# Copies and accumulating transfers of a weight sum moved from the gate and up stage into the attention, and two direct pieces of the down projection moved among the wide pairs

## The chip, the cores and the metric

One core of a Trainium2 chip runs the kernel. The metric is the device time of one execution in microseconds (us). Engines are named as in the profile: PE is TensorE (matmuls; PEld are its weight loads), DVE is VectorE, ACT is ScalarE, POOL is GpSimd, SP is SyncE, which here only issues DMAs. Each engine runs its instructions in the order in which they stand in the program.

## What is computed

One encoder layer over 272 tokens (256 and 16 meta tokens) with two parallel groups of attention heads, then a gated MLP with a depthwise convolution of width 3. In outline, with what doesn't matter here left out:

```python
hn = rmsnorm(h, mix_norm_g)
proj = hn @ w_in                                 # 2048 columns in
q_a, k_a, v_a, cq, ckv, k_pe = split(proj)
out_a = neighbourhood_attention(q_a, k_a, v_a)   # 8 heads of 128
out_b = mla_attention(cq, ckv, k_pe)             # 8 heads, low rank, rotary key
h = h + concat(rmsnorm(out_a), rmsnorm(out_b)) @ w_out
x = rmsnorm(h, ffn_norm_g)
g, u = x @ w_gate, x @ w_up                      # 2048 x 5632 each
gc = conv_b + sum(conv_w[i] * shifted(g, i) for i in range(3))
h = h + (silu(gc) * u) @ w_down                  # 5632 x 2048
return h[N_META:]
```

## The kernel before

Everything is float32. PE multiplies in a shorter format, so each weight tile `raw` is split into a high part `whi` (ACT, line 249) and a low part `wlo` (DVE, line 253, `raw - whi`), and activations likewise (`hl` for hidden states, `act` for MLP values). A product is then two or three matmuls: `mm3` (lines 712 to 714) takes three, `mm2` (lines 2035 and 2036) two, of which the first is 512 columns wide.

Weights come in **pieces** of 128 x 1024 (512 KB), in one list `pieces` that sets the order for the whole kernel: a load on SP into one of five or six `raw` buffers, a split into one of four `whi` and `wlo` buffers, and the products. A `raw` buffer is free when DVE has written `wlo`, and only then SP can issue the next load. The stages by the span's time: input projections and attention to about 285 us, output projection (`w_out`) to about 375, gate and up to about 945, and the down projection to the end; the profile's marks for them are the tile names `in_w_in`, `in_w_out`, `in_w_gate`, `in_w_up` and `in_w_down`.

Parts of up and down use a scheme with seven products for a 2 x 2 block product instead of eight. It needs sums of quarters of the activation, which are saved to DRAM and loaded again (`s_up`, `s_down`, into `sin`, `sums` or a part of `act`), and sums of quarters of the weights (`weight_sums`). `RowPair` is one pair of 128-row blocks in such a group. There are three kinds: five groups of four column tiles in up (`in_w_up_s`), the `mid` group of down (512 columns, `in_w_down_m`), and the **wide group** (the first 1024 columns of down, `in_w_down_s`), with 22 pairs of four pieces each. The last 512 columns of down are **direct pieces** (`others` in the code, `in_w_down` in the profile): four column tiles of 44 blocks, six pieces each, 24 in all, with `mm2` for the first three tiles and `mm3` for the last.

For the wide group one or two of the weight sums are not made by DVE but in DRAM, ahead of time (`early` tiles, 22 of them, 512 KB and 256 KB in turn). For each, SP issues a **copy** of one or two quarters from the weights in DRAM to the tile (line 776), and when that has landed POOL issues an **adding transfer** (line 781) that accumulates another quarter onto it. Both were issued by one generator, `sums_in_dram`, started in `mlp_buffers` at the beginning of gate and up (line 1888). The wide group's pairs then load the tiles like weights.

What sets the order is a planner, `Flow`: each part of the kernel is a generator that asks for an engine with a cost in ns, the planner keeps a clock for each engine, always serves the request that can start first, and writes the instruction into the program at that moment. A transfer is modelled in `load` as bytes at 350 a ns behind all earlier ones (`dma_free`) and a fixed latency. So the order on each engine is fixed when the program is built, and a constant such as `EARLY_PACE`, the planner's pause between two steps of `sums_in_dram`, moves instructions.

The order of the MLP's pieces is the list `work`. Ahead of the wide group's pairs stand the last mid pieces and the first direct pieces, in the order of the string `TAIL` (m is a mid piece, d a direct one); `BEHIND` direct pieces stand behind the pairs, and the rest is spread among them:

```python
    ahead = others[:AHEAD]
    work += [(left if c == "m" else ahead).pop(0) for c in TAIL]
    n = len(others) - BEHIND
    work += spread(scheme, others[AHEAD:n])
    work += others[n:]
```

`spread` puts the last of the pieces that it spreads behind the last pair's piece. After that pair `scheme_out` combines the seven products on ACT, DVE and POOL and sends the result out, while PE works on the direct pieces behind.

## Time and profile before

| | us |
|---|---|
| median of 3 runs | 1115.56 |
| lowest and highest | 1112.71, 1118.1 |
| the profiled execution | 1116.94 |
| its span on the core | 1114.8 |

The span runs from the first to the last instruction of the program; 2.1 us of the execution lie around it. In rows of the profile, `L253 DVE TENSOR_TENSOR wlo<-raw,whi 128x512` is an instruction of line 253 on DVE that writes `wlo` from `raw` and `whi`; buffer numbers are left out. A row with `PE bank L289 <- DVE wlo L253` says that PE's instruction waited, and what it waited for. SPq and POOLq are the issues of DMAs; a `q` behind a number in the DMA view is a hardware queue (q1 is fed by SP, q0 by POOL). Idle time of an engine matters only where PE in the end waits for it.

### The profile page before, as it was taken

How to read it: one execution, taken by the hardware profiler on the slowest of the kernel's cores; microseconds unless marked ns; L12 is line 12 of the kernel's file. 1: busy time of each engine (PE TensorE's matmuls, PEld its weight loads, DVE VectorE, ACT ScalarE, POOL GpSimd, SP SyncE). 2: the span in 40 equal slices, each digit the busy share in tenths (PEclk: the TensorE clock that was granted, in tenths of full speed). 3: DMA queues.
4: the chain of work that ended last, by engine and by line, in shares of the span. 5: the costliest groups of instructions: out<-in, count | busy, mean ns of one | idle time of the engine just before them, and what ended most of it. 6: DMA issues, size and time to landing. Idle time of an engine off the chain costs nothing.

```text
span 1114.8 us, 22339 instructions
## 1 busy us (share of the span) xinstructions
PE 1102.8 (99%) x8164; PEld 1049.1 (94%) x8164; DVE 1015.9 (91%) x1922; ACT 751.8 (67%) x1514; POOL 142.8 (13%) x217
## 2 busy tenths in 40 slices
PE   9999999999999999999999999999999999999998
PEld 9999999999999999999999999999999999887777
DVE  7979888888878989999999999999999989899997
ACT  8788989898647786556656556666665665676664
POOL 3211222121332300000000000000000000310011
PEclk9999999999999999999999999999999999999999
DMA  9653434444655689778868878889889879698891
GB/s 318 197 174 121 151 123 156 139 155 140 225 185 171 216 308 306 250 244 244 288 196 268 253 239 267 284 253 316 296 295 304 269 271 360 241 316 298 296 315 75
DMA packets 82470, 265.35 MB, mean 238 GB/s; under 512 B 9304, under 2 KB 13016, under 8 KB 82360
## 3 DMA queue, kind: packets, MB, share of 16 engines
q1 hardware_dynamic: 78600, 254.08, 66.9%
q0 software_dynamic: 3472, 9.57, 4.9%
q8 instruction: 64, 1.05, 0.4%
q14 instruction: 46, 0.38, 0.1%
q10 hardware_dynamic: 288, 0.27, 0.1%
HBM read 245.39 MB, written 35.13 MB: 252 GB/s over the span
## 4 chain that ended last, share of the span: by engine, by line
PE 62%; DVE 21%; DMA 7%; ACT 5%; issue 4%; POOL 0%; SPq 0%; DVEq 0%; ACTq 0%; POOLq 0%
PE bank L289 14%; DVE wlo L253 12%; PE bank L714 11%; PE bank L712 11%; PE bank L713 11%; PE bank L2035 8%; PE bank L2036 4%; DMA raw<-in_w_up_s 3%; ACT whi L249 3%; DVE raw L253 2%; PE bank L295 2%; DVE mt L253 2%; DMA halves<-early 1%; DVE halves L253 1%; DVE mt L261 1%
## 5 line engine op out<-in xcount | busy, mean ns | idle before, releaser
L249 ACT ACTIVATE whi<-raw 128x512 fp32r<-128x512 f32 (+2 forms) x512 | 381.5, 766 | 159.9 <-PE bank L713 48.1
L253 DVE TENSOR_TENSOR wlo<-raw,whi 128x512 fp32r<-128x512 f32 (+2 forms) x512 | 443.5, 885 | 33.1 <-ACT whi L249 31.7
L712 PE MATMUL bank<-hl,whi 128*128 128x258 f32 (+1 forms) x1208 | 348.5, 289 | 0.1
L714 PE MATMUL bank<-hl,wlo 128*128 128x258 f32 (+1 forms) x1208 | 345.1, 286 | 1.4 <-DVE wlo L253 1.3
L713 PE MATMUL bank<-hl,whi 128*128 128x258 f32 (+1 forms) x1208 | 344.3, 285 | 0.0
L714 PEld LDWEIGHTS bank<-hl,wlo 128*128 128x128 f32 x1208 | 230.4, 191 | 3.5 <-DVE wlo L253 2.9
L713 PEld LDWEIGHTS bank<-hl,whi 128*128 128x128 f32 x1208 | 230.1, 190 | 0.1
L712 PEld LDWEIGHTS bank<-hl,whi 128*128 128x128 f32 x1208 | 229.2, 190 | 0.8 <-ACT scr L249 0.3
L289 PE MATMUL bank<-whi,act 128*128 128x256 f32 (+1 forms) x600 | 153.2, 306 | 0.6 <-ACT whi L249 0.6
L2035 PE MATMUL bank<-hl,whi 128*128 128x512 f32 x384 | 136.5, 395 | 0.0
L289 PEld LDWEIGHTS bank<-whi,act 128*128 128x128 f32 x600 | 105.1, 189 | 7.0 <-ACT whi L249 0.8
L2036 PE MATMUL bank<-hl,wlo 128*128 128x256 f32 x384 | 107.6, 280 | 0.0
L289 PE MATMUL bank<-wlo,act 128*128 128x256 f32 (+1 forms) x300 | 92.3, 308 | 1.4 <-DVE wlo L253 1.4
L2035 PEld LDWEIGHTS bank<-hl,whi 128*128 128x128 f32 x384 | 72.2, 188 | 14.8
L249 ACT ACTIVATE whi<-halves 128x1024 fp32r<-128x1024 f32 (+1 forms) x68 | 63.7, 948 | 32.3 <-PE bank L289 17.5
L253 DVE TENSOR_TENSOR wlo<-halves,whi 128x1024 fp32r<-128x1024 f32 (+1 forms) x68 | 74.1, 1113 | 4.2 <-ACT whi L249 4.2
L289 PE MATMUL bank<-whi,sin 128*128 128x256 f32 (+1 forms) x264 | 76.6, 333 | 0.0
L2036 PEld LDWEIGHTS bank<-hl,wlo 128*128 128x128 f32 x384 | 72.4, 188 | 0.0
L781 POOL DMA_DIRECT2D early<-in_w_down_s x22 | 18.2, 826 | 374.0 <-DMA early<-in_w_down_s 359.4
L249 ACT ACTIVATE whi<-more_raw 128x1024 fp32r<-128x1024 f32 (+2 forms) x59 | 49.6, 856 | 23.2 <-PE bank L2035 7.5
L289 PEld LDWEIGHTS bank<-wlo,act 128*128 128x128 f32 x300 | 56.7, 189 | 5.3 <-DVE wlo L253 2.2
L253 DVE TENSOR_TENSOR wlo<-more_raw,whi 128x1024 fp32r<-128x1024 f32 (+2 forms) x59 | 57.0, 980 | 2.0 <-ACT whi L249 2.0
(309 smaller groups left out, 2151.2 us busy)
## 6 DMA issues: line engine op xcount, KB each, us to landing
raw<-in_w_gate SPq DMA_DIRECT2D x71, 512.0 KB, 5.6
raw<-in_w_in SPq DMA_DIRECT2D x52, 512.0 KB, 4.0
raw<-in_w_up SPq DMA_DIRECT2D x42, 512.0 KB, 5.0
raw<-in_w_up_s SPq DMA_DIRECT2D x33, 512.0 KB, 6.1
raw<-in_w_out SPq DMA_DIRECT2D x32, 512.0 KB, 3.9
sin<-s_down SPq DMA_DIRECT2D x30, 512.0 KB, 7.1
s_down<-sums SPq DMA_DIRECT2D x22, 512.0 KB, 6.9
raw<-in_w_down_m SPq DMA_DIRECT2D x18, 512.0 KB, 6.2
```

The lines of the kernel that those rows point to most:

```text
L249: nc.scalar.activation(out, in_, f, **kw)
L253: nc.vector.tensor_tensor(out, a, b, op)
L261: nc.vector.scalar_tensor_tensor(out, a, s, b, op0, op1)
L289: nc.tensor.matmul(o, l, r, start=start, stop=stop)
L295: nc.tensor.transpose(o, i, ident[:n, :n])
L712: nc.tensor.matmul(ps, whi, xhi, start=start, stop=False)
L713: nc.tensor.matmul(ps, whi, xlo, start=False, stop=False)
L714: nc.tensor.matmul(ps, wlo, xhi, start=False, stop=stop)
L781: nc.gpsimd.dma_start(t, src, accum_op=ALU.add)
L2035: nc.tensor.matmul(ps, whi, x, start=start, stop=False)
L2036: nc.tensor.matmul(ps[:, :n], wlo, x[:, 0, :], start=False, stop=stop)
```

## The change

`sums_in_dram` is split in two. `copies_in_dram` issues the 22 copies on SP with a pause of 6000 in the planner's clock, from when the 15th piece has landed; `sums_in_dram` issues the 22 adding transfers on POOL with a pause of 9500, from when the 49th has. Both are started by `first_loads`, in the attention, and no longer by `mlp_buffers`. The string `TAIL` loses its last d, so 8 and not 9 direct pieces stand ahead of the wide pairs, and `BEHIND` is 3 and not 4, so 13 and not 11 are spread among the pairs. What is computed stays the same.

```diff
-EARLY_PACE = 15000.0
+EARLY_PACE = 9500.0
+COPY_PACE, COPY_AT, SUMS_AT = 6000.0, 14, 48
 LANDING, SAVING = 2600.0, 2500.0
-BEHIND = 4
-MID_LEAD, TAIL = 4, "mmdmmddddmmdddd"
+BEHIND = 3
+MID_LEAD, TAIL = 4, "mmdmmddddmmddd"
...
+    copied = [Event() for _ in early]
+
+    def copies_in_dram():
+        for (t, src, _, _), ev in zip(early, copied):
+            yield "sp", 600
+            load(t, src, ev, nc.sync)
+            fl.cur.t += COPY_PACE
+
     def sums_in_dram():
-        copied = [Event() for _ in early]
-        for i in range(len(early) + 2):
-            if i < len(early):
-                t, src, _, _ = early[i]
-                yield "sp", 600
-                load(t, src, copied[i], nc.sync)
-            if i >= 2:
-                t, _, src, done = early[i - 2]
-                yield copied[i - 2]
-                yield "pool", 1000
-                nc.gpsimd.dma_start(t, src, accum_op=ALU.add)
-                dma_free[0] = max(dma_free[0], fl.cur.t) + 8 * P * size(t) / 350.0
-                fl.set(done, 8000.0)
+        for (t, _, src, done), ev in zip(early, copied):
+            yield ev
+            yield "pool", 1000
+            nc.gpsimd.dma_start(t, src, accum_op=ALU.add)
+            dma_free[0] = max(dma_free[0], fl.cur.t) + 8 * P * size(t) / 350.0
+            fl.set(done, 8000.0)
             fl.cur.t += EARLY_PACE
...
         load(mb, io["meta_bias"], Event(), nc.sync)
+        yield pieces[COPY_AT].loaded
+        fl.spawn(copies_in_dram())
+        yield pieces[SUMS_AT].loaded
+        fl.spawn(sums_in_dram())
...
         fl.set(ev_mlp)
-        fl.spawn(sums_in_dram())
```

SP in the attention, at the second head pair (`scr` from `scr` is the exchange of halves for the rotary embedding, `bias` the attention bias), before:

```order
L542 DMA raw_84<-in_w_in 128x1024
L542 DMA raw_80<-in_w_in 128x1024
L542 DMA bias_191<-in_na_bias 128x544
L542 DMA scr_179<-scr_180 32x258 x4
L542 DMA bias_192<-in_na_bias 128x544
L542 DMA raw_81<-in_w_in 128x1024
L542 DMA raw_82<-in_w_kv_up 128x512
L542 DMA raw_83<-in_w_in 128x1024
```

and now:

```order
L543 DMA raw_84<-in_w_in 128x1024
L543 DMA early_146<-in_w_down_s 128x512
L543 DMA raw_80<-in_w_in 128x1024
L543 DMA bias_191<-in_na_bias 128x544
L543 DMA scr_179<-scr_180 32x258 x2
L543 DMA early_147<-in_w_down_s 128x1024
L543 DMA scr_179<-scr_180 32x258 x2
L543 DMA bias_192<-in_na_bias 128x544
L543 DMA raw_81<-in_w_in 128x1024
L543 DMA raw_82<-in_w_kv_up 128x512
L543 DMA early_148<-in_w_down_s 128x512
```

Copies stand between the weight loads, and one of 512 KB between the two halves of the exchange; the weight loads keep their order.

POOL in the attention, at the softmax rows (`p`) of the second head pair, before:

```order
L277 TENSOR_TENSOR p_185<-p_185 128x16
L277 TENSOR_TENSOR sq8r_213<-sq_211,sq8r_213 128x4
L277 TENSOR_TENSOR p_186<-p_186 128x16
L277 TENSOR_TENSOR p_187<-p_187 128x16
L277 TENSOR_TENSOR p_185<-p_185 128x16
L277 TENSOR_TENSOR p_186<-p_186 4x16
L277 TENSOR_TENSOR sum_b<-sum_b,scr_181 128x258
L277 TENSOR_TENSOR p_185<-p_185 128x16
```

and now:

```order
L278 TENSOR_TENSOR p_185<-p_185 128x16
L278 TENSOR_TENSOR sq8r_213<-sq_211,sq8r_213 128x4
L278 TENSOR_TENSOR p_186<-p_186 128x16
L783 DMA early_135<-in_w_down_s 128x1024
L278 TENSOR_TENSOR p_187<-p_187 128x16
L278 TENSOR_TENSOR p_185<-p_185 128x16
L278 TENSOR_TENSOR p_186<-p_186 4x16
L783 DMA early_136<-in_w_down_s 128x512
L278 TENSOR_TENSOR sum_b<-sum_b,scr_181 128x258
L278 TENSOR_TENSOR p_185<-p_185 128x16
```

The 22 adding transfers stand among this work, the first ones here; the last stands among the sums of squares of the residual at the end of the output projection.

SP at the end of the program, before:

```order
L542 DMA halves_11124<-early_156 128x512
L542 DMA halves_11124<-in_w_down_s 128x512
L542 DMA halves_11164<-in_w_down 128x1024 x2
L542 DMA sin_5412<-s_down_134 128x1024
L542 DMA halves_11043<-in_w_down 128x1024
L542 DMA halves_11086<-in_w_down 128x1024
L542 DMA raw_82<-in_w_down 128x512
```

and now:

```order
L543 DMA sums_93<-s_down_133 128x1024
L543 DMA halves_11043<-in_w_down_s 128x512
L543 DMA halves_11043<-in_w_down 128x1024
L543 DMA halves_11164<-in_w_down 128x1024
L543 DMA halves_11086<-in_w_down 128x1024
L543 DMA sin_5456<-s_down_134 128x1024
L543 DMA more_raw_5458<-in_w_down 128x512
```

Behind the last piece of a pair stand four direct pieces (`in_w_down`) and no longer five.

## The prediction

> **What bounds the kernel now.** I read the head of the page first, then the table of busy time by stretches of the span, then the waits of each engine in the stretches that the change touches, then the chain of waits and the DMA view.

> ```profile
> span 1114.8 us, 22339 instructions
> PE 1102.8 (99%) x8164; PEld 1049.1 (94%) x8164; DVE 1015.9 (91%) x1922; ACT 751.8 (67%) x1514; POOL 142.8 (13%) x217
> ```

> TensorE (PE) is busy 99% of the span, so the most that any reordering can return is what PE loses to waits. The table of stretches (length, then busy time of PE, PEld, DVE, ACT, POOL, then clock, DMA share, GB/s) says where that is:

> ```profile
> 33.00:138.00 105.00, 104.23 (x844) 101.99 (x843) 90.52 (x241) 88.55 (x268) 18.87 (x43) 1.00 0.49 157
> 138.00:372.00 234.00, 233.93 (x1945) 232.42 (x1944) 202.43 (x482) 178.62 (x499) 61.10 (x92) 1.00 0.50 163
> 400.00:780.00 380.00, 376.84 (x2920) 365.14 (x2919) 361.72 (x670) 233.62 (x376) 18.18 (x22) 1.00 0.84 266
> 780.00:950.00 170.00, 170.00 (x1241) 161.44 (x1240) 157.98 (x275) 103.22 (x160) 0.00 (x0) 1.00 0.87 299
> 950.00:984.00 34.00, 33.09 (x164) 27.37 (x163) 30.73 (x36) 22.14 (x30) 10.21 (x10) 1.00 0.72 252
> 984.00:1098.00 114.00, 112.29 (x518) 90.22 (x517) 111.64 (x125) 75.81 (x85) 9.62 (x8) 1.00 0.83 284
> ```

> PE is idle for 3.16 us in 400 to 780, where the copies and adds in DRAM now run, for none in 780 to 950, the rest of gate and up without them, and for 1.71 us in the wide pairs (984 to 1098), where DVE is busy 111.64 of 114 us. In the attention (33 to 372) it is idle for 0.84 us of 339, at a DMA share of 0.5. The waits of 400 to 780 (us in total, times, longest):

> ```profile
> PE bank L289 <- DVE wlo L253: 1.4, 3, 0.9
> PE bank L714 <- DVE wlo L253: 1.0, 5, 0.3
> PE bank L289 <- ACT whi L249: 0.6, 1, 0.6
> DVE raw L253 <- DMA raw<-in_w_up_s: 7.0, 6, 2.0
> ACT whi L249 <- DMA raw<-in_w_gate: 7.9, 5, 3.4
> ACT whi L249 <- DMA raw<-in_w_up_s: 4.5, 5, 2.1
> ```

> PE waits nine times, nearly always for a split weight; behind it DVE and ACT wait for weights to land. In 780 to 950 the same view lists no wait of PE and none on a weight load. One case followed through, from the chain of waits and PE's timeline:

> ```profile
> 583.67 8.09 DMA more_raw<-in_w_up_s
> 591.78 0.70 DVE raw L253
> ...
> 596.05 0.39 PE L714 MATMUL bank<-hl,wlo 128*128 128x258 f32 x1 [0.32 <-DVE wlo L253]
> ```

> A weight load takes 8.09 us, DVE starts its sums only then, and 4 us later PE stands still for its `wlo`. A stall costs more than its idle time:

> ```profile
> 1065.94 0.63 PE L289 MATMUL bank<-whi,sin 128*128 128x512 f32 x2
> 1066.79 0.50 PE L289 MATMUL bank<-wlo,sin 128*128 128x512 f32 x1 [0.22 <-DVE wlo L253]
> 1067.13 0.40 PE L289 MATMUL bank<-whi,sin 128*128 128x512 f32 x1
> 1067.36 0.39 PE L289 MATMUL bank<-whi,act 128*128 128x512 f32 x1
> ```

> From 1065.94 to 1067.13 are three starts, which at the pitch of the last two (0.23) take 0.69 us and took 1.19: 0.50 us lost for 0.22 shown, so 0.28 more per stall. In 400 to 780 PE thus loses 3.16 + 9 x 0.28 = **5.7 us**.

> **The copies and adds leave gate and up.** The DMA view of 400 to 780, and behind it one row of the same view of 60 to 300:

> ```profile
> q1 hardware_dynamic: 26064, 92.02, 70.0%
> q0 software_dynamic: 3096, 8.54, 13.7%
> raw<-in_w_gate SPq DMA_DIRECT2D x50, 512.0 KB, 6.0
> ...
> raw<-in_w_in SPq DMA_DIRECT2D x40, 512.0 KB, 3.9
> ```

> The adds (q0) take 13.7% of 380 us, 52 us of all 16 DMA engines. The copies are as many bytes on q1; at its mean rate, 8.54/92.02 of 70.0%, 6.5% or 25 us. Without both the share of 0.84 falls to about 0.64. That lies between 780 to 950 (0.87) and the attention (0.50), where loads of the same size land in 3.9 us and not 6.0. The gain is between nothing (the stretch 780 to 950 has the higher share and no stall, so share alone isn't the cause) and 5.7 us. What 780 to 950 lacks is bursts that other queues push in front of a load that DVE needs next, and that is what is removed; but DVE stays busy 361.72 of 380 us, and some stalls are its own. I take three quarters: **-4.3 us**. What would be late next is DVE.

> **They enter the attention.** By the rows they stand between, SP issues the 22 copies from about 33 to 180 us and POOL the adds from about 138 to 372. The copies wait for no buffer; what stands behind one on SP and in the hardware queue is the next weight load, the bias or the rope exchange. A copy of 512 KB is 25 us / 16.5 = 1.5 us of all engines (8.54 MB are 16.5 times 512 KB), an add 52 / 16.5 = 3.2 us. So the share becomes 0.5 + 25/147 = 0.67 up to 180 and about 0.72 in 138 to 372. Does anything there wait for a load? In 33 to 372 the view of the tile `raw` lists these, with no DMA row among what its engines waited for:

> ```profile
>   PE bank L713: 22.6, 27
> DMA to landing us min/median/max: 2.6/3.9/7.0
> ```

> Splits start late because `whi` is still in use by PE (22.6 us), not because weights are late, so a load that comes 1.5 to 3 us later is covered by that. The cover is thin only near 33 to 48 us, where the prefetch has not built up; four copies (two of 512, two of 256 KB) are placed there, 4.5 us of the queue. Bounds for the attention on SP: 0 to 4.5 us; near the lower end, since one load in three or four meets a copy: +0.3.

> POOL gets the 22 adds in front of attention work. In gate and up the view of the tile `early` gives one issue 0.81 us; now the rows of POOL in 33 to 372, of PE there, and of DVE in 138 to 372:

> ```profile
> L781 POOL DMA_DIRECT2D early<-in_w_down_s x22: 805/812/1011, 407.1 to 776.7; - x22
> ...
> POOL p L277 <- ACT p L249: 60.7, 29, 7.6
> ...
> PE bank L289 <- POOL sq8r L277: 0.5, 2, 0.3
> ...
> L257 DVE TENSOR_SCALAR p<-p,cols 128x272 f32<-128x272 f32 x22 | 7.8, 354 | 0.8
> ```

> Before its softmax rows (`p`) POOL is idle 60.7/29 = 2.1 us on average, waiting for ACT, so an issue of 0.81 fits. What is behind an issue is the copy of meta columns of `p`, which PE's transposes wait for, and the small sums `sq8r`, for which PE already waits twice (0.5 us). The adds wait for copies a hundred us older, so for nothing. Bounds: 0 to 22 x 0.81 = 17.9 us; near the lower end by the 2.1 us: +0.2. Attention together: **+0.5 us**.

> [...]

> **Two direct pieces move.** One leaves the run before the wide pairs and one the run behind them; both go among the pairs. A direct piece is 8 blocks; in the wide stretch PE's starts are 0.35 us apart per block, and DVE's split of one piece is in the third row:

> ```profile
> 1060.26 0.40 PE L2035 MATMUL bank<-act,whi 128*128 128x512 f32 x1
> 1060.61 0.39 PE L2035 MATMUL bank<-act,whi 128*128 128x512 f32 x1
> L253 DVE TENSOR_TENSOR wlo<-halves,whi 128x1024 fp32r<-128x1024 f32 x37 | 45.4, 1245 | 0.7 <-ACT whi L249 0.7
> PE bank L289 <- DVE wlo L253: 1.6, 4, 0.6
> ```

> PE gets 2.8 us of work for 1.25 us of DVE, 1.55 us of relief for a stretch that DVE bounds; two give 3.1. The loss there is 1.71 + 4 x 0.28 = 2.8 us (the last row is its waits), so the gain is 0 to 2.8; not all, because a piece helps only the pairs next to it and adds 512 KB to queues at 0.83: **-2.0 us**. In 950 to 984, where PE is idle 0.91 us and DVE 3.3 of 34, one piece of cover is gone: between 0 and 1.55, near 0 because DVE has 3.3 us free: **+0.2 us**.

> Behind the pairs:

> ```profile
> 1097.63 0.28 PE L712 MATMUL bank<-act,whi 128*128 128x256 f32 x1
> 1110.47 0.28 PE L714 MATMUL bank<-act,wlo 128*128 128x256 f32 x1
> 1099.37 0.69 DVE L253 TENSOR_TENSOR raw<-bank,more_raw 128x512 f32<-128x512 f32 x1
> 1105.42 2.20 DVE L261 SCALAR_TENSOR_TENSOR raw<-raw,s,resT 128x256 f32<-128x256 f32 x4
> 1111.70 0.33 SPq L2024 DMA_DIRECT2D outT<-mt  x1
> ```

> Five direct pieces (36 blocks, 108 matmuls from 1097.63 to 1110.47, 0.36 us a block) hide the combination of the seven products, which ends on DVE at 1107.62, 10.0 us after the last pair. Four pieces (28 blocks) leave 10.1 us, and one split of 1.25 us fewer stands between the combining steps, so it ends near 8.8. Cover is left: 0 us; if DVE were 2 us late there, 0.7 us would show.

> **The sum:** -4.3 + 0.5 - 2.0 + 0.2 + 0 = -5.6 us. The profiled execution took 1116.94 (span 1114.8 and 2.1 around it) and would take 1111.3; it lies 1.4 above the median 1115.56, from which the forecast is **1110.0 us**.

> **Rivals.** *The stalls of gate and up are DVE's own.* For it: DVE busy 95% there; stalls also follow runs of DVE work with no load in the chain. Against: 7.0 us of DVE's 18.3 idle ended with one kind of load. Then -4.3 becomes about -0.5, and the sum is -1.8: 1113.8 us.

> *The adds hold POOL back in the attention* (slower than before). [...] For it: PE waits for POOL already; POOL runs in order. Against: 2.1 us of idle time per softmax row. [...]

> *All losses of both stretches go,* 5.7 + 2.8, and the attention costs nothing: 1107 us. For it: the clean 780 to 950. Against: DVE at 95 to 98%.

> **How the numbers follow.** Forecast 0.50 (own range 1107.5 to 1113.5), DVE's stalls 0.18, POOL on the path 0.17, all gone 0.15. A change of 0.5% (5.6 us, below 1110.0 or above 1121.1) is about what a measurement here can tell. Faster by that: all of the last case and half of the forecast's, whose middle lies on the bound: 0.40. Slower: most of the POOL case and a remainder for mixtures with the SP bound of 4.5: 0.17. Within: 0.43. The range for 8 in 10 is 1104.5 to 1118: it holds the first, second and last case and cuts most of the POOL case.

> **What would show it.** In the changed profile: no wait of DVE or ACT for loads of `in_w_up_s` or `in_w_gate` above 1 us in all in 400 to 780, DMA share near 0.64 and PE idle below 1 us there; in the attention no row of PE waiting for POOL or for a DMA above 0.5 us, and issues of adds below 1.2 us; in the wide pairs PE idle below 1 us; the last pair some 10 us before PE's end and the last combining step before that end. The forecast is wrong if gate and up keeps its waits with the share down (then DVE sets them), or if PE's idle time in 33 to 372 grows beyond 3 us.

## The result, and the profile after

| us | before | change |
|---|---|---|
| median | 1115.65 (4 runs, 1112.71 to 1118.10) | 1108.12 (4 runs, 1107.54 to 1108.52) |
| the profiled execution | 1116.94 | 1107.99 |
| its span | 1114.8 | 1106.0 |

The ratio is 0.9933, with a 95% interval of 0.9913 to 0.9952: 7.5 us less, where 5.6 were forecast. First the head of the page of the changed kernel and its table of stretches (columns as before: length, busy time of PE, PEld, DVE, ACT, POOL, clock, DMA share, GB/s):

```profile
span 1106.0 us, 22349 instructions
PE 1095.7 (99%) x8164; PEld 1046.2 (95%) x8164; DVE 1016.9 (92%) x1922; ACT 750.8 (68%) x1514; POOL 149.6 (14%) x217
```

```profile
33.00:138.00 105.00, 104.10 (x845) 102.05 (x844) 90.51 (x241) 88.18 (x268) 20.26 (x43) 1.00 0.66 214
138.00:372.00 234.00, 233.84 (x1945) 232.52 (x1944) 201.70 (x482) 177.85 (x497) 76.82 (x113) 1.00 0.76 211
...
400.00:780.00 380.00, 380.00 (x2979) 370.40 (x2978) 369.74 (x683) 239.08 (x386) 0.00 (x0) 1.00 0.68 226
780.00:950.00 170.00, 170.00 (x1229) 160.89 (x1228) 158.05 (x273) 102.39 (x158) 3.90 (x4) 1.00 0.85 296
950.00:984.00 34.00, 34.00 (x160) 27.84 (x159) 33.77 (x36) 23.73 (x28) 6.10 (x6) 1.00 0.85 304
984.00:1098.00 114.00, 110.00 (x543) 90.89 (x542) 107.46 (x121) 72.00 (x85) 20.06 (x10) 1.00 0.75 255
```

In 400 to 780 PE is never idle now (3.16 us before), and DVE got through 683 instructions instead of 670 in the same time. The view of waits of that stretch no longer has a row of PE, nor one of DVE or ACT on `in_w_gate` or `in_w_up_s`. In 950 to 984 the idle 0.91 us are gone too. In the wide pairs PE is idle for more than before: 4.00 us against 1.71. The attention stands at DMA shares of 0.66 and 0.76, up from 0.5, and PE's idle time there grew only from 0.84 to 1.06 us.

Idle time doesn't show all that PE loses, so I also measured from start to start: for each kind of matmul (line and shape) the time from one start to the next, less the median of that kind, summed over a stretch. On before that gives 20.8 us in all, on the change 12.0; the difference, 8.8, is that of the two spans. In us, by stretch:

| start-to-start loss of PE | 0–100 | 100–400 | 400–800 | 800–950 | 950–1000 | 1000–1100 |
|---|---|---|---|---|---|---|
| before | 5.4 | 1.9 | 8.4 | -0.1 | 1.2 | 4.1 |
| change | 4.8 | 1.8 | -0.1 | 0.0 | 0.2 | 5.3 |

So gate and up gave 8.5 us, about the whole gain of the two profiled executions (8.8). The rest moved by 1.2 us at most in either direction. How kinds of matmuls are grouped moves such a sum by some 0.3 us, and each is of one execution: the run that moves only the pieces (below) has the order of before up to 928 us and lost 6.5 us in 400 to 800, not 8.4.

### The profile page after: what moved, and what is told of

Same layout as the page of the kernel before. It is cut to its first block, busy times and chain, and to the rows that moved or that the text cites. A ratio compares the mean times of both kernels' runs of the same rounds, so it can differ in the third digit from the quotient of the medians.

```text
span 1106.0 us, 22349 instructions
## 1 busy us (share of the span) xinstructions
PE 1095.7 (99%) x8164; PEld 1046.2 (95%) x8164; DVE 1016.9 (92%) x1922; ACT 750.8 (68%) x1514; POOL 149.6 (14%) x217
## 4 chain that ended last, share of the span: by engine, by line
PE 83%; DVE 7%; ACT 4%; DMA 3%; issue 2%; POOL 0%; DVEq 0%; SPq 0%; ACTq 0%; POOLq 0%
PE bank L290 23%; PE bank L713 15%; PE bank L714 15%; PE bank L715 15%; PE bank L2040 10%; PE bank L2041 5%; DVE wlo L254 4%; PE bank L296 2%; ACT whi L250 1%; DMA raw<-early 1%; DVE scr L262 1%; ACT scr L250 1%; DMA raw<-in_w_cq 1%; DMA halves<-early 1%; DVE halves L254 1%
## 5 line engine op out<-in xcount | busy, mean ns | idle before, releaser
L713 PE MATMUL bank<-hl,whi 128*128 128x258 f32 (+1 forms) x1208 | 347.7, 288 | 0.0
L714 PE MATMUL bank<-hl,whi 128*128 128x258 f32 (+1 forms) x1208 | 343.7, 285 | 0.0
L714 PEld LDWEIGHTS bank<-hl,whi 128*128 128x128 f32 x1208 | 229.3, 190 | 0.1
L713 PEld LDWEIGHTS bank<-hl,whi 128*128 128x128 f32 x1208 | 228.3, 189 | 0.4
L278 POOL TENSOR_TENSOR mt<-mt,mt 128x256 f32<-128x256 f32 x3 | 13.5, 4496 | 646.6 <-ACT mt L250 646.6
## 6 DMA issues: line engine op xcount, KB each, us to landing
raw<-in_w_gate SPq DMA_DIRECT2D x74, 512.0 KB, 4.8
raw<-in_w_in SPq DMA_DIRECT2D x52, 512.0 KB, 4.9
raw<-in_w_up SPq DMA_DIRECT2D x43, 512.0 KB, 4.9
raw<-in_w_up_s SPq DMA_DIRECT2D x34, 512.0 KB, 4.4
raw<-in_w_out SPq DMA_DIRECT2D x32, 512.0 KB, 5.3
sin<-s_down SPq DMA_DIRECT2D x30, 512.0 KB, 6.5
s_down<-sums SPq DMA_DIRECT2D x22, 512.0 KB, 4.4
raw<-in_w_down_m SPq DMA_DIRECT2D x18, 512.0 KB, 5.5
```

The lines of the kernel that those rows point to most:

```text
L278: nc.gpsimd.tensor_tensor(out, a, b, op)
L713: nc.tensor.matmul(ps, whi, xhi, start=start, stop=False)
L714: nc.tensor.matmul(ps, whi, xlo, start=False, stop=False)
```

## The experiments

Each table row gives the median, the ratio to the kernel before on the same chip with its interval, and the same loss of PE in the three stretches in question (the last one from 950 us to the end). The medians of before beside these runs lay between 1114.64 and 1115.33 us.

| run | us | ratio | 100–400 | 400–800 | from 950 |
|---|---|---|---|---|---|
| before | 1115.65 | | 1.9 | 8.4 | 5.3 |
| change | 1108.12 | 0.9933 [0.9913, 0.9952] | 1.8 | -0.1 | 5.5 |
| only the sums moved | 1108.61 | 0.9940 [0.9924, 0.9955] | 2.8 | -0.1 | 6.0 |
| only the pieces moved | 1115.08 | 0.9999 [0.9987, 1.0011] | 1.9 | 6.5 | 4.0 |
| only TAIL, with the sums | 1109.62 | 0.9949 [0.9934, 0.9965] | 2.5 | -0.2 | 6.6 |
| before, no adds | 1108.76 | 0.9944 [0.9927, 0.9961] | 1.9 | 0.9 | 4.2 |
| before, no copies, no adds | 1108.51 | 0.9940 [0.9916, 0.9964] | 1.7 | 1.0 | 4.8 |
| before, copies early | 1112.07 | 0.9966 [0.9953, 0.9979] | 2.3 | 4.4 | 6.6 |
| change, adds late | 1140.06 | 1.0225 [1.0202, 1.0248] | 2.1 | 32.9 | 5.1 |
| change, no copies, no adds | 1107.41 | 0.9931 [0.9914, 0.9947] | 1.8 | -0.2 | 5.9 |
| change, adds dense | 1123.99 | 1.0074 [1.0050, 1.0098] | 18.4 | -0.1 | 4.5 |
| THIRD = 1 | 1108.22 | 0.9941 [0.9925, 0.9956] | 5.6 | -0.2 | 2.2 |
| THIRD = 1, old pieces | 1108.13 | 0.9940 [0.9923, 0.9957] | 5.7 | -0.2 | 2.7 |
| THIRD = 1, same order | 1107.64 | 0.9942 [0.9927, 0.9958] | 4.5 | -0.2 | 1.8 |

**Which part of the change.** The change with the old pieces, and before with the new pieces:

```diff
-BEHIND = 3
-MID_LEAD, TAIL = 4, "mmdmmddddmmddd"
+BEHIND = 4
+MID_LEAD, TAIL = 4, "mmdmmddddmmdddd"
```

> Only the copies and the adding transfers are moved, as in the change; TAIL and BEHIND stay as before. Theory A, from the two profiles: gate and up lost about 8 us to these transfers and all of it comes back, while the move of the two direct pieces is worth nothing or less. Then this kernel takes 1107 to 1108.5 us, no longer than the change (1108.1). Theory B, the prediction's terms: the pieces earn 2 us of their own, and this kernel takes 1110 us or more; PE idle time in the wide pairs is then well above that of the change (4.0 us).

> Only TAIL and BEHIND are changed; copies and adds stay in gate and up. Theory A: the same 3 us of PE idle time in 400 to 780 us as before, and a time of 1115 to 1117 us. Theory B: 1113 to 1114 us. Also asked: whether the dip of the granted clock to 0.50 at 663 to 666 us, just behind two stalls of PE of 0.62 and 0.88 us, comes again in this execution, since the order up to there is the same.

Moving only the sums takes 1108.61 us, and moving only the pieces changes nothing that can be told: by the interval (0.9987 to 1.0011) at most 1.4 us faster. The sums are the whole gain as far as the runs resolve it; the pieces' expected 2 us is not there. A third run kept BEHIND at 4 and took only TAIL from the change:

> As the change, but BEHIND stays 4: one direct piece less ahead of the pairs and one more among them. The stall of PE for a low part of a direct piece at about 970 us (0.9 us, in before and in the run with only the sums moved, gone in the change) tells which of the two moves took it away: gone here if it was TAIL. Time 1107.5 to 1109 us either way.

It took 1109.62 us, a little more than expected, and the stall behind 950 us stays with it (PE waits 1.15 us for a `wlo` of a direct piece at 959 us). So TAIL alone didn't remove it; it is gone in the runs that have TAIL and BEHIND both as in the change, and also in the run with THIRD = 1 and the old pieces (below). BEHIND alone wasn't run.

**Copies or adds.** Three kernels keep the order of before on PE, DVE, ACT and, the adds aside, POOL, and leave out or displace transfers. The first drops the adds:

```diff
-                nc.gpsimd.dma_start(t, src, accum_op=ALU.add)
+                pass
```

> As before, but the adding transfers are left out (the early sums keep only the copied quarter, so the wide group's output is another); every other instruction stands in the same order. If the adds make the stalls: 1107.5 to 1109 us and no wait of DVE for weights in 400 to 780. If the copies do: 1114 to 1116. If the stalls are DVE's own: 1115 with PE idle for about 3 us as before.

The second drops the copies as well; the planner still counts their bytes:

```diff
-        early_sums.append((t, ev))
+        early_sums.append((early[-1][1], ev))
...
-                load(t, src, copied[i], nc.sync)
+                left_out(t, copied[i])
...
```

> As before, but copies and adding transfers are both left out; the wide pairs load the plain quarter of the weights in place of the early sum, as many bytes (their output is another). All other instructions stand in the same order. Theory A (the adds alone make the stalls): as without the adds, 1108.8 us, within 1.5. If the copies had a share of their own: 1105 to 1107. It also gives the floor of gate and up: loss of PE in 400 to 800 below 0.5 us by A, about 1 us (as without the adds) if its last stall is DVE's own.

The table of stretches of before without the adds, and then of before without both:

```profile
400.00:780.00 380.00, 379.12 (x2971) 369.47 (x2970) 368.50 (x681) 239.29 (x384) 0.00 (x0) 1.00 0.74 249
```

```profile
400.00:780.00 380.00, 379.11 (x2971) 369.36 (x2970) 368.49 (x681) 240.02 (x384) 0.00 (x0) 1.00 0.68 226
```

The copies show as 0.06 of the DMA share (23 us of all engines; 25 were estimated) and cost nothing: 2971 matmuls and 0.9 us of idle time in both. That one stall, for a `wlo` at 654 us, remains with no extra transfer at all, so it belongs to the order of before. The change, whose order on DVE and ACT is another there, doesn't have it, with its transfers or without: about 1.0 of the 8.5 us came with the order, 7.4 with the transfers.

For the opposite case, adds without copies, I first left the adds in gate and up and moved only the copies:

```diff
-EARLY_PACE = 9500.0
+EARLY_PACE = 15000.0
...
-        yield pieces[SUMS_AT].loaded
-        fl.spawn(sums_in_dram())
...
         fl.set(ev_mlp)
+        fl.spawn(sums_in_dram())
```

> As the change, but the adding transfers are issued in gate and up at the old pace, only the copies in the attention. If the adds (52 of the 77 us of all engines that both took there) make the stalls: 1112 to 1115 us, with waits of DVE and ACT for weights in 400 to 780. If the copies do, which stand in the same queue as the weights: 1108 to 1109 us. If both share by their bytes on the engines: 1113.

As a test of that it missed. All 22 adds were issued from 384.8 to 453.3 us, because nothing that they wait for came later: the planner's pause orders instructions, it doesn't hold one back. Its waits in 400 to 780 (engine, line, awaited: us in total, times, longest) show what such a burst does:

```profile
POOL early L783 <- issue: 42.8, 17, 3.1
ACT whi L250 <- DMA raw<-in_w_gate: 17.0, 5, 5.2
ACT whi L250 <- DMA raw<-in_w_up: 11.2, 3, 7.4
PE bank L2039 <- ACT whi L250: 11.2, 2, 9.4
```

Loads of weights came so late that PE once stood still for 9.4 us, and the granted clock was 0.50 for 27 us of that stretch; 1140 us. The mended run copies all bytes in the attention and repeats one row of each copy at its old place, so that each add is held as before:

```diff
-                load(t, src, copied[i], nc.sync)
+                load(t[:1], src[:1], copied[i], nc.sync)
...
         load(mb, io["meta_bias"], Event(), nc.sync)
+        yield pieces[14].loaded
+        fl.spawn(copies_in_dram())
```

> As before, but the bytes of the copies move in the attention; at the old place of each copy only its first row is copied once more, so that each adding transfer waits as before and is issued at its old place in gate and up. PE, DVE and POOL keep their order. It mends the run with the late adds, where nothing held the adds back and 22 went out within 70 us. If the adds alone make the stalls: 1113 to 1116, as before, with 5 us or more of lost PE time in 400 to 780. If it takes copy and add together to fill the queues: 1109 to 1111.

1112.07 us, between the two answers. Above the floor of 1.0 us, adds alone lose 3.4 us in gate and up, copies alone none, both together 7.4, 1.5 of it at half clock (below); in the run with only the pieces moved, both together lose 5.5. The medians agree: against the 1108.51 us without transfers, copies alone cost 0.3 us, adds alone (with their small copies) 3.6, both 6.8. So adds are dear, and copies cost something only beside them. Waits of this run in 400 to 780; the first of before was 7.9 us, the second 7.0:

```profile
ACT whi L249 <- DMA raw<-in_w_gate: 7.0, 4, 3.0
DVE raw L253 <- DMA raw<-in_w_up_s: 3.7, 4, 1.6
```

The DMA view of 400 to 780 says the same by the median landing of a 512 KB load of `in_w_gate`: 6.0 us before, 5.5 with adds alone, 4.9 with copies alone, 4.7 with neither, and 4.3 in the change:

```profile
raw<-in_w_gate SPq DMA_DIRECT2D x54, 512.0 KB, 4.3
```

**What the attention pays.** The change with copies and adds left out:

```diff
-        early_sums.append((t, ev))
+        early_sums.append((early[-1][1], ev))
...
-            load(t, src, ev, nc.sync)
+            left_out(t, ev)
...
-            nc.gpsimd.dma_start(t, src, accum_op=ALU.add)
+            pass
```

> As the change, but with the copies and adding transfers left out of the attention; the wide pairs load the plain quarter instead (their output is another). Theory A: the attention hides both wholly, and this kernel takes what the change takes, 1108.1 us, within 1; the loss of PE in 33 to 372 stays about 2.5 us. Rival, the prediction's term for the attention: 0.5 us less or more. If POOL or the SP queue cost something there that the two profiles hide: 1104 to 1106.

1107.41 against 1108.12 us, with overlapping ranges, and the same 1.8 us of loss in 100 to 400: the attention hides them, up to 0.7 us that these runs don't resolve. The view of `raw` in 33 to 372 of the change fits this, the first row being what ACT waited for:

```profile
  PE bank L714: 22.6, 27
...
DMA to landing us min/median/max: 2.7/5.0/8.8
```

Loads there land 1.1 us later than before (median 5.0 against 3.9), and the 22.6 us in which ACT waits for PE to free a `whi`, the cover that the prediction named, stand unchanged.

How near is the edge? With the adds as dense as the copies allow:

```diff
-EARLY_PACE = 9500.0
+EARLY_PACE = 1500.0
```

> As the change, but the pause between two adding transfers is 1500 and not 9500 of the planner's clock: they follow each other as fast as the copies land, between about 137 and 185 us, up to three between two softmax rows. The rival of the prediction (adds hold POOL back in the attention) at its strongest: each issue of 0.8 us, some three in a row, in front of the copies of meta columns; half of 22 on the path would be 1117 us or more. If ACT's lateness hides them (POOL idle 2.1 us a row): 1108 to 1109.5. Bursts in the queues of the weights, as in the run with late adds: 1120 or more.

16 us are lost. Of its waits from 130 to 250:

```profile
POOL early L783 <- issue: 16.8, 10, 3.6
PE bank L290 <- POOL sq8r L278: 2.8, 2, 2.1
PE bank L296 <- POOL p L278: 2.0, 2, 1.6
```

POOL stood idle before 17 of the adds, 31 us in all; where the view says "issue", it names nothing that POOL waited for. The landings of earlier adds do. From the traces of this run and of the one with late adds (us):

| run, add | POOL idle before it | issued | landing of the add three places ahead | of the one eight places ahead |
|---|---|---|---|---|
| dense, 5th | 3.60 | 150.42 | 150.17 | |
| dense, 6th | 1.69 | 152.94 | 152.69 | |
| dense, 9th | 0.45 | 163.38 | 163.06 | 144.96 |
| dense, 12th | 2.54 | 175.08 | 174.77 | 155.44 |
| dense, 20th | 1.92 | 199.31 | 199.00 | 183.44 |
| late, 4th | 6.42 | 393.90 | 393.65 | |
| late, 22nd | 2.98 | 453.31 | 453.00 | 435.43 |

In the dense run 16 adds, and in the late one all 19 from the fourth on, are issued 0.25 to 0.32 us after the add three places ahead has landed, and there are never more than three under way. The program's own waits don't ask for that: an add waits for its copy and, from the ninth on, for the add eight places ahead, which had landed 13 us earlier or more. So in these runs a fourth add holds POOL until one of three has landed. Whether the limit counts transfers or their bytes (512 and 256 KB in turn) isn't shown.

Issued every 3.5 us (22 from 136.7 to 209.9), the adds thus held POOL, and the softmax rows and small sums behind them, for which PE waits, came late. How much of the 16 us that makes isn't shown: PE's rows for POOL give 4.8 us, some 4.6 us were lost at half clock (186.1 to 189.5 and 213.4 to 220.3 us), the DMA engines were full (share 1.07 in the row below), and from 146 us on the planner's order of PE, DVE and ACT is another than in the change.

```profile
170.00:190.00 20.00, 16.64 (x124) 16.01 (x124) 14.00 (x28) 14.93 (x47) 8.44 (x14) 0.91 1.07 280
```

The rival of the prediction stands here at another density. At the change's pace of some 11 us at most two adds are under way, and the same view of the change has one such wait, of 0.2 us.

**A version beyond both.** With THIRD = 1 every early sum has two quarters: DVE makes 11 sums of 0.6 us less, and the attention carries 5.6 MB more.

```diff
-THIRD = 2
+THIRD = 1
```

> As the change, but THIRD = 1: all 22 early sums hold two quarters (512 KB), so in 11 pairs DVE makes two sums and not three, while copies and adds each move 11 times 256 KB more in the attention, and the pairs load 2.8 MB more. If the attention still hides them and the wide stretch is bound by DVE: 11 sums of 0.61 us less for DVE, of which PE gets back up to the 5 us that it loses in 984 to 1098: 1103.5 to 1107. If the adds of 512 KB no longer fit their pace (each of them then waits for one eight places earlier): slower, with PE waiting for POOL in 138 to 372. If the loads bound the wide stretch: 1108 to 1111.

> As the run with THIRD = 1, but TAIL and BEHIND as before, so two direct pieces fewer among the pairs. If the pieces are worth nothing, as in the runs that moved only one part: the same time within 1 us. If DVE has become free in the wide stretch, pieces among the pairs are not needed there: equal or up to 1 us faster.

1108.22 us, above the 1103.5 to 1107 of a hiding attention, and 1108.13 with the old pieces, the same within 1 us as expected. The wide pairs then lose 2.2 us instead of 5.3, which fits that DVE's sums bound them, and 100 to 400 loses 3.8 us more. To see whether that came with the planner's new order, the longer transfers were counted at their old bytes:

```diff
...
-            load(t, src, ev, nc.sync)
+            load(t, src, ev, nc.sync, 1 + g % 2)
...
```

> As the run with THIRD = 1, but the planner counts the 11 longer copies and adds at their old bytes, so that up to the wide pairs PE, DVE, ACT and POOL keep exactly the order of the change. In the run with THIRD = 1 PE lost 3.1 us less in 1000 to 1100 than in the change, and 3.4 us more in 150 to 400. If that second loss came with the planner's new order there: 1104.5 to 1106 us, the loss in 150 to 400 back at about 1 us. If it came with the 5.6 MB more of copies and adds in the queues and on POOL: 1107.5 to 1109 again, with the loss at the same places.

The wide pairs lose 1.4 us, and 2.0 of the 4.5 us in the attention are one stall that begins at 184 us and ends at 186.5, when DVE has written `late`; in the chain that follows some 4 us of DVE's work on an exchange of halves on SP's queue, which landed 8.43 us after its issue:

```profile
173.83 8.43 DMA scr<-scr
```

1107.64 us: its range (1106.47 to 1110.88) covers the change's, so none of the three is shown to beat it. Longer early sums with the exchange kept clear of copies weren't tried.

## Why the prediction was right, and where its terms were not

**Gate and up, forecast -4.3, measured -8.5.** The mechanism was right: the signs it named came (no wait on `in_w_gate` or `in_w_up_s` in 400 to 780, PE idle 0, share 0.68 for the forecast 0.64), and the runs without transfers show that 7.4 us of it are the transfers and about 1.0 the new order. The size was off at the step that made 5.7 us of the 3.16 us of idle time, "0.28 more per stall", and called it the bound. From start to start, the eleven gaps of that stretch that lost over 0.15 us lose 5.0 us with 3.16 idle, so 0.17 more per gap, not 0.28. But 1.5 us went at half clock behind two of them, and 1.9 in starts that came late without any gap in the view. The view of waits already listed PEld waiting for `wlo`; I didn't count that. Taking three quarters of the wrong bound made it smaller still.

**The attention, forecast +0.5, measured between 0 and 0.7.** The cover behind `whi` and POOL's idle time held; PE's waits for POOL grew from 0.5 to 0.7 us in all. An add's issue took 1.02 us at most, below the 1.2 named as a sign:

```profile
L783 POOL DMA_DIRECT2D early<-in_w_down_s x22: 602/825/1020, 136.6 to 371.7; - x22
```

Its median of 0.825 us among the softmax rows stands beside 0.812 in gate and up. Only three of the 22 issues overlapped a TENSOR_SCALAR or cast of DVE in time (0.814, 0.841 and 0.989 us), and the longest overlapped none. The 1.2 us, which also stands behind the 0.17 for POOL on the path, was an estimate: 0.81 for an issue and 0.354 for one `TENSOR_SCALAR` that it waits for. No run shows such a wait; the change shows issues of 0.60 to 1.02 us, and with three overlaps it hardly puts the wait to the test.

**The pieces, forecast -2.0 + 0.2, measured nothing.** This step failed, and so did the sign named for it: PE is idle for 4.00 us in the wide pairs, not below 1. In the change the wide pairs lose 1.2 us more and the front 1.0 us less; with only the pieces moved 0.3 and 0.9 less, and the median doesn't follow. "1.55 us of relief" per piece assumed that PE's stall and DVE's lead add up over the stretch. The waits of the change in 984 to 1098 show single late splits instead. The two longest stalls, 1.12 and 1.08 us, stand in the chain of waits behind loads of early sums that took 7.65 and 7.30 us:

```profile
PE bank L290 <- DVE wlo L254: 4.0, 5, 1.1
DVE more_raw L254 <- DMA halves<-early: 2.3, 1, 2.3
DVE halves L254 <- DMA raw<-early: 1.5, 1, 1.5
```

Fewer sums for DVE helped there (5.3 to 1.4 us), a direct piece elsewhere in the row of pairs did not. Why the front's stall went only with both constants, where THIRD is 2, is open.

**The tail, forecast 0, measured 0.** The last pair's last matmul and the last one of PE, and the last combining step on DVE:

```profile
1091.50 0.39 PE L290 MATMUL bank<-whi,sin 128*128 128x512 f32 x1
1101.69 0.28 PE L715 MATMUL bank<-act,wlo 128*128 128x256 f32 x1
```

```profile
1098.51 2.20 DVE L262 SCALAR_TENSOR_TENSOR halves<-halves,s,resT 128x256 f32<-128x256 f32 x4
```

From the end of the pair at 1091.7, PE has 10.2 us of cover (10.1 forecast) and the combining ends after 9.0 (8.8).

That the sum came out near is in part luck: gate and up gave 4.2 us more than forecast, the pieces 1.8 less. The measured 1108.12 us lies nearer to the third rival's 1107 than to the forecast's 1110.0. The first rival fell (stalls that stay without any transfer are 1.0 us of the 8.4). The second fell at this pace and came true in part at a denser one. The third, all losses gone at 1107, was right for gate and up and wrong for the wide pairs.

## What to carry to other kernels

Look for a stage whose loads are early before placing background transfers: here the same bytes cost 7.4 us where DVE waits for loads, and at most 0.7 where splits wait for PE. The attention also had the lower DMA share, so these runs don't tell the two apart; no transfers were moved into 780 to 950, which had a share of 0.87 and no stall. In these runs a pause in the plan didn't pace a queue (with a pause of 15000 ns, 22 adds went out within 69 us); what held a transfer back was a wait or the work in front of it, and 22 of them let loose cost 16 to 32 us. In the dense and the late run a fourth add also stopped the engine that was to issue it, for up to 6.42 us, until one of three under way had landed. Before idle time is turned into a gain, measure the loss from start to start: idle gaps were 3.2 of 8.4 us here.

## What was unexpected of the hardware

In five of the 14 profiled executions stalls of PE were followed by a granted clock of 0.50. The table of stretches of before, in single us, behind the two stalls of 0.62 and 0.88 us that end at 661.4:

```profile
661.00:662.00 1.00, 0.64 (x5) 0.64 (x6) 1.00 (x2) 0.58 (x2) 0.00 (x0) 1.00 0.81 328
662.00:663.00 1.00, 1.00 (x9) 1.00 (x9) 1.00 (x3) 0.98 (x4) 0.00 (x0) 0.81 0.11 45
663.00:664.00 1.00, 1.00 (x7) 1.00 (x7) 1.00 (x4) 0.75 (x1) 0.00 (x0) 0.50 0.33 98
664.00:665.00 1.00, 1.00 (x6) 1.00 (x6) 1.00 (x1) 0.00 (x0) 0.00 (x0) 0.50 1.04 283
665.00:666.00 1.00, 1.00 (x7) 1.00 (x6) 0.96 (x4) 0.00 (x0) 0.00 (x0) 0.50 0.83 324
666.00:667.00 1.00, 1.00 (x10) 1.00 (x10) 0.97 (x3) 0.98 (x2) 0.00 (x0) 0.98 0.91 254
```

For 3.4 us the clock is 0.50, which costs 1.5 us from start to start, as much as the two stalls are idle. The run with only the pieces moved has the same pair of stalls and the same dip. The run with the adds alone has the same pair too (0.62 and 0.88) and no dip, which is 1.5 of the 1.9 us of difference between them in 650 to 700. A single stall of 1.75 us was followed by one (change without transfers, 1044 us), one of 1.53 us was not (before without transfers, 1046 us).
